# Attention scores on one core: two batches interleaved per transpose, 8 KB load runs, all loads ahead of all stores

## The chip, the cores and the metric

One core of a Trainium2 chip. The metric is device time in microseconds; the profile's span is 1.8 to 2 us shorter. Short names: PE is TensorE, DVE is VectorE, ACT is ScalarE, POOL is GpSimd, SP is SyncE, which here issues all DMAs. A slice of the page is a fortieth of the span, and a digit in it is a busy share in tenths.

## The reference

```python
batch, heads, seq, dim = 8, 8, 512, 64            # q, k: float32
def reference(q, k):
    scale = 1.0 / np.sqrt(q.shape[-1])
    return (np.einsum('bhqd,bhkd->bhqk', q, k) * scale).astype(np.float32)
```

16.78 MB come in, 67.11 MB go out.

## The kernel before

Each batch is loaded, cast to bf16, transposed on TensorE, which puts the 64 dims on the partitions, multiplied and evicted from PSUM with the scale. One transpose takes a 128 x 128 block made of two halves of the heads (index x), 64 dims each, so x later picks the upper or lower 64 rows of TensorE (the profile has the score matmuls as 64*64). Loads run four batches ahead; from then on each batch's stores are mixed with the loads of a later one.

```python
    G = H // 2; M = P // G; R = S // M; RO = 8          # 4, 32, 16
    q_r = q.rearrange("b (x g) (m j) d -> b (g m) x (j d)", x=2, j=R)   # two runs of 4 KB per partition
    raw_pool = ...(name="raw", bufs=4)    # kf and qf, 8 KB each per partition
    bf_pool  = ...(name="bf", bufs=2)     # kb and qb
    t_pool   = ...(name="t", bufs=2)
    out_pool = ...(name="out", bufs=6)    # 16 KB per partition, 2 MB each
    # tpsum: 2 tiles, psum: 3 tiles
    ...
    for b in range(B):
        ... casts of kf, qf (GpSimd; VectorE and ScalarE for the first batch)
        for j0 in range(0, R, 8):
            tp = tpsum_pool.tile([P, 8, P], bf16, name="tp")
            ... 8 transposes of kb into tp
            nc.vector.tensor_copy(out=kT[:, :, j0:j0 + 8], in_=tp.rearrange("d j p -> d p j"))
        ... the same for qb, evicted by ScalarE into qT
        for g0 in range(0, G, 2):
            os = [out_pool.tile([P, 2 // HP, RO, S], f32, name="o") for _ in range(2)]
            ... 32 matmuls (64 rows, 64 columns, 512 wide), evictions by turns on ScalarE and VectorE
            for x in range(2):
                nc.sync.dma_start(out=out_r[b, x, ...], in_=os[x]...)      # 16 KB runs
            if g0 == 0 and b + AHEAD < B:
                load(b + AHEAD)
```

The two tiles written together are called a pair here: 4.19 MB of stores, 16 pairs in all. ScalarE evicts into the first tile of a pair, VectorE into the second.

## Time and profile before

| | before |
|---|---|
| time, median of 3 | 206.02 us (205.98 to 206.03) |
| span | 204.0 us |
| busiest compute engine | TensorE, 63% of the span |
| DMA queue, share of 16 engines' span | 97.6% |
| moved | 83.89 MB in 16 loads and 32 stores |

Read the row of DMA shares first: here it is full from end to end (a 9, that is 90% or more, in 38 of 40 slices), while the busiest compute engine has 63%. So I take the DMA as the bound, and its own rate in GB/s by stage is what counts. The list of DMA issues says how deep the queue is (count, KB each, median us from issue to landing; the line of the stores):

```profile
out_dram<-o SPq DMA_DIRECT2D x32, 2048.0 KB, 24.8
```

A 2 MB store alone takes 4.9 us, by my estimate, at the 430 GB/s of the stretch with stores only (120 to 195 us). At 24.8 us from issue to landing, about five stores are queued at any time. That depth goes with the six output tiles; with the four of the changed kernel its page has 14.4 us, three stores.

### The profile page before, as it was taken

What the parts mean: (1) busy time and instruction counts of PE and PEld (TensorE: products, weight loads), DVE (VectorE), ACT (ScalarE), POOL (GpSimd) and SP (SyncE); (2) the same over time, 40 slices, a digit from 0 to 9 for tenths busy, and PEclk for the clock granted to TensorE, in tenths of its full rate; (3) what the DMA queues carried; (4) which work ended last, traced back from release to release, by engine and by line L of the source; (5) the groups of instructions that cost most, each with busy time, mean ns of one, the idle gap of its engine ahead of it and who ended that gap; (6) DMA issues with size and microseconds to landing.
All of it is one profiled execution on the core that took longest, in us unless ns stands there. A gap on an engine that the chain in (4) does not pass through costs nothing.

```text
span 204.0 us, 1911 instructions
## 1 busy us (share of the span) xinstructions
PE 128.7 (63%) x768; PEld 44.1 (22%) x768; DVE 94.4 (46%) x82; ACT 82.8 (41%) x83; POOL 29.0 (14%) x34
## 2 busy tenths in 40 slices
PE   0398877774969559696586955959787777600000
PEld 0353433260103411033110431103211111000000
DVE  0459895912639035490536705367628081800000
ACT  2477888263522625227252452527552525200000
POOL 1077530520006100070001600000000000000000
PEclk9999999666555855558555575555555555555555
DMA  5999999999999999999999999999999999999991
GB/s 204 419 409 411 439 427 404 441 434 424 437 400 432 440 421 419 434 429 427 440 407 414 438 427 437 427 421 437 424 430 437 426 434 424 430 437 427 434 408 61
DMA packets 8969, 84.01 MB, mean 412 GB/s; under 512 B 768, under 2 KB 768, under 8 KB 4864
## 3 DMA queue, kind: packets, MB, share of 16 engines
q1 hardware_dynamic: 8960, 83.89, 97.6%
q8 instruction: 6, 0.10, 0.2%
q14 instruction: 3, 0.02, 0.0%
HBM read 16.78 MB, written 67.11 MB: 411 GB/s over the span
## 4 chain that ended last, share of the span: by engine, by line
DMA 61%; DVE 14%; PE 6%; ACT 6%; issue 1%; SPq 0%; DVEq 0%
DMA out_dram<-o 57%; DVE o L73 11%; PE ps L119 4%; ACT o L71 4%; DMA qf<-in_q_dram 3%; DVE kT L97 3%; ACT qT L105 1%; PE tp L103 1%; PE tp L95 0%; DVE qb L87 0%; SPq L56 0%; SPq L128 0%; DVEq L73 0%
## 5 line engine op out<-in xcount | busy, mean ns | idle before, releaser
L119 PE MATMUL ps<-kT,qT 64*64 64x512 bf16 x512 | 103.1, 556 | 38.6 <-ACT o L71 24.9
L73 DVE TENSOR_SCALAR o<-ps 128x1024 f32<-128x1024 f32 x64 | 75.2, 1219 | 76.7 <-DMA out_dram<-o 56.8
L71 ACT ACTIVATE o<-ps 128x1024 f32<-128x1024 f32 x64 | 64.5, 1025 | 77.1 <-PE ps L119 65.7
L119 PEld LDWEIGHTS <-qT 64*64 64x64 bf16 x512 | 22.4, 124 | 111.5 <-issue 108.6
L87 POOL CAST kb<-kf 128x1024 bf16<-128x1024 f32 x14 | 14.2, 1040 | 80.9 <-DMA kf<-in_k_dram 80.3
L105 ACT COPY qT<-tp 128x1024 bf16<-128x1024 bf16 x16 | 16.1, 1015 | 12.6 <-PE tp L103 12.4
L97 DVE COPY kT<-tp 128x1024 bf16<-128x1024 bf16 x16 | 18.9, 1215 | 0.0
L95 PE MATMUL tp<-identity,kb 128*128 128x128 bf16 x128 | 12.4, 257 | 8.0 <-ACT kb L87 6.9
L103 PE MATMUL tp<-identity,qb 128*128 128x128 bf16 x128 | 14.9, 284 | 2.2 <-DVE kT L97 1.4
L87 POOL CAST qb<-qf 128x1024 bf16<-128x1024 f32 x14 | 14.2, 1040 | 6.4 <-DMA qf<-in_q_dram 6.4
L103 PEld LDWEIGHTS <-qb 128*128 128x128 bf16 x128 | 11.7, 130 | 9.6 <-issue 8.6
L95 PEld LDWEIGHTS <-kb 128*128 128x128 bf16 x128 | 10.4, 118 | 11.4 <-ACT kb L87 6.9
L87 DVE CAST kb<-kf 128x1024 bf16<-128x1024 f32 x1 | 0.7, 694 | 5.8 <-DMA kf<-in_k_dram 5.8
L87 ACT CAST kb<-kf 128x1024 bf16<-128x1024 f32 x1 | 1.0, 1044 | 3.8 <-DMA kf<-in_k_dram 3.8
L87 ACT CAST qb<-qf 128x1024 bf16<-128x1024 f32 x1 | 1.0, 1044 | 1.5 <-DMA qf<-in_q_dram 1.5
L87 ACT ACT_TABLE_LOAD x1 | 1.3, 1283 | 0.7 <-PEq L147 0.7
L87 DVE CAST qb<-qf 128x1024 bf16<-128x1024 f32 x1 | 0.7, 695 | 1.9 <-DMA qf<-in_q_dram 1.9
masks.py:199 POOL TENSOR_SCALAR_AFFINE_SELECT identity<-identity 128x128 bf16<-128x128 bf16 x1 | 0.3, 292 | 0.1
masks.py:197 POOL MEMSET identity<- 128x128 bf16 x1 | 0.2, 204 | 0.3 <-POOLq L147 0.3
L147 POOL MEMSET const-float32-0.0<- 128x1 f32 x1 | 0.1, 98 | 0.2 <-issue 0.2
L147 POOL MEMSET const-bfloat16-1.0<- 128x1 bf16 x1 | 0.1, 101 | 0.0
L147 POOL MEMSET const-uint8-127<- 128x1 uint8 x1 | 0.1, 101 | 0.0
(1 smaller groups left out, 0.1 us busy)
## 6 DMA issues: line engine op xcount, KB each, us to landing
out_dram<-o SPq DMA_DIRECT2D x32, 2048.0 KB, 24.8
kf<-in_k_dram SPq DMA_DIRECT2D x8, 1024.0 KB, 17.2
qf<-in_q_dram SPq DMA_DIRECT2D x8, 1024.0 KB, 19.6
```

What stands on the lines that cost most here:

```text
L71: nc.scalar.mul(out=dst, in_=src, mul=scale)
L73: nc.vector.tensor_scalar(out=dst, in0=src, scalar1=scale, scalar2=None, op0=mybir.AluOpType.mult)
L87: copy(out=dst[:, :, x, :], in_=slab[:, x].rearrange("p (j d) -> p j d", j=R))
L95: nc.tensor.transpose(out=tp[:, j, :], identity=identity, in_=kb[:, j0 + j].rearrange("p x d -> p (x d)"))
L97: nc.vector.tensor_copy(out=kT[:, :, j0:j0 + 8], in_=tp.rearrange("d j p -> d p j"))
L103: nc.tensor.transpose(out=tp[:, i, jj, :], identity=identity, in_=qb[:, RO * jj + i0 + i].rearrange("p x d -> p (x d)"))
L105: nc.scalar.copy(out=qT[:, i0:i0 + IW], in_=tp.rearrange("d i jj p -> d i p jj"))
L119: nc.tensor.matmul(out=pss[x][h * U:(h + 1) * U, w, :], lhsT=qTh[rows, i + w, g, :], rhs=kTh[rows, g, :], start=True, stop=True, tile_posi ...
L147: nc = _bacc.Bacc("TRN2", target_bir_lowering=False, num_devices=1)
```

## The change

The intent: longer load runs (8 KB instead of two of 4 KB), a queue with all reads ahead of all writes, and the transposed q and k of everything held on chip. To get 8 KB runs, x now means two batches instead of two halves of the heads; two batches are a unit, and there are four units. The memory for this comes from the output tiles, of which 4 are left. Cut to its core:

```diff
-    G = H // 2
+    UNITS = B // 2
+    G = H
-    q_r = q.rearrange("b (x g) (m j) d -> b (g m) x (j d)", x=2, j=R)
+    q_r = q.rearrange("b g (m j) d -> b (g m) (j d)", j=R)
-    raw_pool = ctx.enter_context(tc.tile_pool(name="raw", bufs=4))
-    bf_pool = ctx.enter_context(tc.tile_pool(name="bf", bufs=2))
-    t_pool = ctx.enter_context(tc.tile_pool(name="t", bufs=2))
-    out_pool = ctx.enter_context(tc.tile_pool(name="out", bufs=6))
+    raw_pool = ctx.enter_context(tc.tile_pool(name="raw", bufs=6))
+    bf_pool = ctx.enter_context(tc.tile_pool(name="bf", bufs=3))
+    t_pool = ctx.enter_context(tc.tile_pool(name="t", bufs=UNITS))
+    out_pool = ctx.enter_context(tc.tile_pool(name="out", bufs=4))
... (cast, transposes and matmuls as before, for a unit in place of a batch)
+    cast = [load_and_cast(0)]
+    for v in range(1, UNITS):
+        cast.append(load_and_cast(v))
+
+    ts = [transpose(*cast[0])]
+    scores(0, 0, *ts[0])
+    ts.append(transpose(*cast[1]))
+    scores(0, 1, *ts[0])
+    ts.append(transpose(*cast[2]))
+    ts.append(transpose(*cast[3]))
+    for v in range(UNITS):
+        for n in range(2 if v == 0 else 0, H // 2):
+            scores(v, n, *ts[v])
```

scores(v, n) makes and stores one pair.

More of the change, by code (lines that the diff above doesn't have):

```diff
@@ L30 @@
     RO = 8
-    HP = RO * P // S
-    U = P // HP
+    U = S // RO
     JJ = R // RO
+    IW = 8 // JJ
     f32 = mybir.dt.float32
     bf16 = mybir.dt.bfloat16
-    q_r = q.rearrange("b (x g) (m j) d -> b (g m) x (j d)", x=2, j=R)
-    k_r = k.rearrange("b (x g) (m j) d -> b (g m) x (j d)", x=2, j=R)
-    out_r = out.rearrange("b (x n h) (u i) k -> b x n (h u) i k", x=2, h=HP, i=RO)
+    q_r = q.rearrange("b g (m j) d -> b (g m) (j d)", j=R)
+    k_r = k.rearrange("b g (m j) d -> b (g m) (j d)", j=R)
+    out_r = out.rearrange("b (n h) (u i) k -> b n (h u) (i k)", h=2, i=RO)
     consts = ctx.enter_context(tc.tile_pool(name="consts", bufs=1))
-    raw_pool = ctx.enter_context(tc.tile_pool(name="raw", bufs=4))
-    bf_pool = ctx.enter_context(tc.tile_pool(name="bf", bufs=2))
-    t_pool = ctx.enter_context(tc.tile_pool(name="t", bufs=2))
-    out_pool = ctx.enter_context(tc.tile_pool(name="out", bufs=6))
+    raw_pool = ctx.enter_context(tc.tile_pool(name="raw", bufs=6))
+    bf_pool = ctx.enter_context(tc.tile_pool(name="bf", bufs=3))
+    t_pool = ctx.enter_context(tc.tile_pool(name="t", bufs=UNITS))
+    out_pool = ctx.enter_context(tc.tile_pool(name="out", bufs=4))
     tpsum_pool = ctx.enter_context(tc.tile_pool(name="tpsum", bufs=2, space=bass.MemoryType.PSUM))
     psum_pool = ctx.enter_context(tc.tile_pool(name="psum", bufs=3, space=bass.MemoryType.PSUM))
-    AHEAD = 4
-    raws = {}
-    def load(b):
-        kf = raw_pool.tile([P, 2, R * D], f32, name="kf")
-        qf = raw_pool.tile([P, 2, R * D], f32, name="qf")
-        nc.sync.dma_start(out=kf, in_=k_r[b])
-        nc.sync.dma_start(out=qf, in_=q_r[b])
-        raws[b] = (qf, kf)
-    load(0)
-    identity = consts.tile([P, P], dtype=bf16)
-    make_identity(nc, identity)
-    for b in range(1, AHEAD):
-        load(b)
+    identity = None
     n_evac = 0
@@ L75, in evacuate, with load_and_cast @@
         n_evac += 1
-    for b in range(B):
-        qf, kf = raws.pop(b)
-        kb = bf_pool.tile([P, R, 2, D], bf16, name="kb")
-        qb = bf_pool.tile([P, R, 2, D], bf16, name="qb")
-        for slab, dst in ((kf, kb), (qf, qb)):
+    def load_and_cast(v):
+        both = []
+        for src in (k_r, q_r):
+            xb = bf_pool.tile([P, R, 2, D], bf16, name="xb")
             for x in range(2):
-                if b > 0:
+                xf = raw_pool.tile([P, R * D], f32, name="xf")
+                nc.sync.dma_start(out=xf, in_=src[2 * v + x])
+                if v > 0:
                     copy = nc.gpsimd.tensor_copy
@@ L86, with transpose @@
                     copy = (nc.vector.tensor_copy, nc.scalar.copy)[x]
-                copy(out=dst[:, :, x, :], in_=slab[:, x].rearrange("p (j d) -> p j d", j=R))
+                copy(out=xb[:, :, x, :], in_=xf.rearrange("p (j d) -> p j d", j=R))
+            both.append(xb)
+        return both
+    def transpose(kb, qb):
         kT = t_pool.tile([P, P, R], bf16, name="kT")
@@ L97 @@
             nc.vector.tensor_copy(out=kT[:, :, j0:j0 + 8], in_=tp.rearrange("d j p -> d p j"))
-        IW = 8 // JJ
         for i0 in range(0, RO, IW):
@@ L105, with scores @@
             nc.scalar.copy(out=qT[:, i0:i0 + IW], in_=tp.rearrange("d i jj p -> d i p jj"))
+        return kT, qT
+    def scores(v, n, kT, qT):
         kTh = kT.rearrange("d (g m) j -> d g (m j)", g=G)
         qTh = qT.rearrange("d i (g m) jj -> d i g (m jj)", g=G)
-        for g0 in range(0, G, 2):
-            os = [out_pool.tile([P, 2 // HP, RO, S], f32, name="o") for _ in range(2)]
-            for n in range(2 // HP):
-                for i in range(0, RO, 2):
-                    pss = [psum_pool.tile([P, 2, S], f32, name="ps") for _ in range(2)]
-                    for w in range(2):
-                        for h in range(HP):
-                            g = g0 + n * HP + h
-                            for x in range(2):
-                                rows = slice(x * D, (x + 1) * D)
-                                nc.tensor.matmul(out=pss[x][h * U:(h + 1) * U, w, :],
-                                                 lhsT=qTh[rows, i + w, g, :],
-                                                 rhs=kTh[rows, g, :],
-                                                 start=True, stop=True,
-                                                 tile_position=(x * D, h * U))
-                    for x in range(2):
-                        evacuate(os[x][:, n, i:i + 2, :], pss[x])
-            for x in range(2):
-                n0 = g0 // HP
-                nc.sync.dma_start(
-                    out=out_r[b, x, n0:n0 + 2 // HP].rearrange("n p i k -> p n (i k)"),
-                    in_=os[x].rearrange("p n i k -> p n (i k)"))
-            if g0 == 0 and b + AHEAD < B:
-                load(b + AHEAD)
@@ new lines, in scores @@
+        os = [out_pool.tile([P, RO, S], f32, name="o") for _ in range(2)]
+        for i in range(0, RO, 2):
+            pss = [psum_pool.tile([P, 2, S], f32, name="ps") for _ in range(2)]
+            for w in range(2):
+                for h in range(2):
+                    for x in range(2):
+                        rows = slice(x * D, (x + 1) * D)
+                        nc.tensor.matmul(out=pss[x][h * U:(h + 1) * U, w, :],
+                                         lhsT=qTh[rows, i + w, 2 * n + h, :],
+                                         rhs=kTh[rows, 2 * n + h, :],
+                                         start=True, stop=True,
+                                         tile_position=(x * D, h * U))
+            for x in range(2):
+                evacuate(os[x][:, i:i + 2, :], pss[x])
@@ new lines, in scores @@
+        for x in range(2):
+            nc.sync.dma_start(out=out_r[2 * v + x, n], in_=os[x].rearrange("p i k -> p (i k)"))
+    cast = [load_and_cast(0)]
+    identity = consts.tile([P, P], dtype=bf16)
+    make_identity(nc, identity)
+    for v in range(1, UNITS):
[9 more added lines that the diff above has]
+            scores(v, n, *ts[v])
```

## The prediction

> **What bounds the kernel now.** I read the page's slices first, then the table of stretches, the waits, the timeline of the queue and the chain. Slices:
>
> ```profile
> PE 128.7 (63%) x768; PEld 44.1 (22%) x768; DVE 94.4 (46%) x82; ACT 82.8 (41%) x83; POOL 29.0 (14%) x34
> ...
> PEclk9999999666555855558555575555555555555555
> DMA  5999999999999999999999999999999999999991
> GB/s 204 419 409 411 439 427 404 441 434 424 437 400 432 440 421 419 434 429 427 440 407 414 438 427 437 427 421 437 424 430 437 426 434 424 430 437 427 434 408 61
> ```
>
> No slice between the first and the last has the DMA engines under 90% busy, while no compute engine passes 63% of the span. So the time is the bytes over the rate, plus a start and an end. The table of stretches (us; busy and count of each engine; granted clock; DMA share; GB/s) splits that sum. The first 8 loads are queued by 7 us and no store is issued before 18.89, so 5 to 19 is pure load; the last loads land before 120, so 120 to 195 is pure store:
>
> ```profile
> 0.00:5.00 5.00, 0.00 (x0) 0.00 (x0) 0.00 (x0) 1.28 (x1) 0.70 (x6) 1.00 0.59 201
> ...
> 5.00:19.00 14.00, 9.84 (x94) 6.24 (x97) 9.14 (x9) 8.23 (x9) 6.34 (x7) 1.00 1.02 413
> 120.00:195.00 75.00, 42.97 (x196) 9.85 (x195) 30.53 (x26) 25.67 (x26) 0.00 (x0) 0.52 1.01 430
> ...
> 198.00:199.00 1.00, 0.00 (x0) 0.00 (x0) 0.00 (x0) 0.00 (x0) 0.00 (x0) 0.50 0.73 311
> 199.00:200.00 1.00, 0.00 (x0) 0.00 (x0) 0.00 (x0) 0.00 (x0) 0.00 (x0) 0.50 0.31 131
> 200.00:201.00 1.00, 0.00 (x0) 0.00 (x0) 0.00 (x0) 0.00 (x0) 0.00 (x0) 0.50 0.27 115
> 201.00:202.00 1.00, 0.00 (x0) 0.00 (x0) 0.00 (x0) 0.00 (x0) 0.00 (x0) 0.50 0.08 33
> 202.00:203.00 1.00, 0.00 (x0) 0.00 (x0) 0.00 (x0) 0.00 (x0) 0.00 (x0) 0.50 0.04 16
> ```
>
> Loads, in runs of 4 KB, go at 413 GB/s; stores, in runs of 16 KB, at 430. 16.78 MB / 413 = 40.6 us and 67.11 / 430 = 156.1 us, together 196.7. The start costs 5 - 201 x 5 / 413 = 2.6 us. That leaves 204.0 - 199.3 = 4.7 us of end, and the last five lines are it: the 16 DMA engines don't finish together, the last is about 4 us behind the first.
>
> Compute is kept waiting by the stores, and not the other way round:
>
> ```profile
> DVE o L73 <- DMA out_dram<-o: 56.8, 11, 8.7
> ...
> 59.17 4.73 DVE L73 TENSOR_SCALAR o<-ps 128x1024 f32<-128x1024 f32 x4 [4.95 <-DMA out_dram<-o]
> 60.45 4.75 PE L119 MATMUL ps<-kT,qT 64*64 64x512 bf16 x20 [0.77 <-DVE o L73]
> ```
>
> The first line is of VectorE's waits (total, times, longest), the others of the timeline: when an output buffer comes free, VectorE fills it with 4 evictions in 4.73 us and the store is issued at once (63.68). At the halved clock 20 score matmuls take 4.75 us, so the 32 of a pair of output tiles take about 7.6, against the 9.75 us in which the queue stores that pair (4.19 MB / 430).
>
> [...]
>
> **The change part by part.**
>
> *Load runs.* From 16 loads of two 4 KB runs per partition to 16 loads of one 8 KB run: bytes and loads are the same, runs go from 4096 to 2048. Fit one run on one engine as a fixed part plus bytes over a rate. 4096 x 16 / 413 GB/s = 158.7 ns, 16384 x 16 / 430 GB/s = 609.6 ns; the slope is 450.9 ns per 12288 bytes, the fixed part 158.7 - 150.3 = 8.4 ns. An 8 KB run is then 309 ns (424 GB/s) for two of 158.7, and each engine has 128 of them: 128 x 8.4 = 1.1 us saved. The cut in the sum is 40.6 to 39.5 us. That is all the DMA work that the change removes. The stores keep size, count (32) and run length.
>
> *Order in the queue.* In the built order all 16 loads stand ahead of the first store. Mixing costs nothing now: 20 to 120 moves 42.6 MB, 9.6 of loads and 33.0 of stores, which at 413 and 430 would take 100.0 us and does take 100. So separating them gains nothing either.
>
> *Compute work.* A unit is now two batches transposed together, so there are 4. Casts: the same elements in instructions twice as long (POOL 1040 ns each before, about 2.0 after; the first unit's on VectorE 1.4 and ScalarE 2.1, twice the rows of 694 and 1044 ns). Transposes stay 256, their evictions 32, the score matmuls 512, the evictions 128. Nothing changes there in sum, and none of it is on the path.
>
> *Buffers.* Output tiles go from 6 to 4 and casts from two pairs to 3 singles. These are the new risk, so I place the start by hand, loads landing every 2.47 us from 5.8 (before's first landing): number 8 at 23, 10 at 28, 16 at 43. Do loads ever stall on their 6 buffers? Load 15 needs the cast of load 9 (landed 25.5, cast at 27.5), load 16 that of load 10 (30.0); the engines then are at load 10, so the queue is never under 4 loads deep. Loads end at 5 + (16.78 - 1.0) / 0.424 = 42.2 us. The first store pair is ready at about 28, the second at about 40, both ahead of that; they keep the queue busy to 42.2 + 2 x 9.75 = 61.7 us.
>
> The third pair is the tight spot. In the built order TensorE does the transposes of the third and fourth unit (128) before it goes on with that pair's matmuls, having done only some 16 of 32. With 2 PSUM tiles the transposes run at the pace of their evictions: per unit 4 x 1.22 on VectorE plus 4 x 1.02 on ScalarE, about 0.9 overlapped, 8.1 us. From the end of the second pair's evictions, 39 on VectorE, ScalarE finishes the eighth set of these at about 55.5. Then 3 more rounds of matmuls and evictions at 1.2 to 2 us each (clock between full and half): the first store of the third pair is issued at 61 to 62.5, and before's first load needed about 1 us from issue to its first bytes. First bytes at 62 to 63.5 against 61.7: a gap of 0.3 to 1.8 us, I take 1.2. This is the only idle time of the queue that I find. From the fourth pair on a buffer freed at T gives a new store at T + 4.73 + about 1.2, while the queue has the other pair, 9.75 us: 3.8 us to spare.
>
> *Sum.* 206.0 - 1.1 (runs) + 1.2 (third pair)[...] = 206.2 us.
>
> **Rivals.** (a) No gap: my hand placing is too slow, as it strings waits of two engines end to end, and matmuls at full clock would leave the store in time. The start of the trace speaks for it (clock 1.00 to 30 us). Then only the runs count: 204.9. (b) Better than that: the lag of the slow DMA engines partly comes from short reads, and the 4.7 us end shrinks with half as many. [...] It would give 203 to 204. (c) A new wait: 4 output tiles are too few[...]. [...] Half a microsecond on each of 16 pairs would give 213. (d) These transposes take 4 us longer than placed, at half clock or behind the GpSimd casts into 3 buffers: 209 to 210.
>
> **Range and chances.** The two computed terms cancel, each about 1 us. I put 30% on (a), 10% on (b), 40% on the gap as placed, 13% on (d), 7% on (c). 2% is 4.1 us: faster needs under 201.9, that is the end gone altogether, which nothing here does (0.03). Slower needs over 210.1, (c) or a bad (d): 0.09. Within 2%: 0.88. The range for 8 in 10 is 203.6 to 209.0.
>
> **What would show it.** Runs: a stretch from 5 to 40 us, now pure load, should have 424 GB/s; 413 would mean that run length does nothing. Order: no store issued before 30 us, and loads landing by about 43. Third pair: a dip of DMA share within 60 to 65 us and nowhere else, with VectorE and ScalarE before it busy on the transposes' evictions, not waiting. Buffers: later DMA share 0.99 or more; shares of 0.95 in every pair would prove (c). End: the time from the first thinning of the DMA to the last byte still 4 to 5 us; 2 or less would prove (b). The whole is wrong if another engine than the DMA ends the chain, or if the rate of pure stores leaves 430.

The sum came to 206.2 us. Terms are cut from it: the 0.1 us for the four tiles, which no trace or run shows, so the terms that still stand come to 206.1. The 8.4 ns per run is an estimate, from the trace's 413 and 430 GB/s. For the end the profile shows only the mean share of the 16 engines, 0.73 falling to 0.04 over the last five lines; that some engines lag behind others is my estimate from that (0.04 of 16 engines for 1 us is 0.64 us of work, about one run of 16 KB at the fit's 609.6 ns).

## The result

The changed kernel took 204.58 us (median of 4 runs, 204.37 to 205.21), the kernel before 206.03 in the same rounds. The ratio is 0.9932 (0.9909 to 0.9956). Ratios are the mean time of one kernel's fast runs over that of the other's of the same rounds, so not quite the ratio of the medians quoted. A difference counts only from 2% on. It is 1.45 us less, where 206.2 was forecast.

The page of the changed kernel, slices:

```profile
PE 134.3 (66%) x768; PEld 40.9 (20%) x768; DVE 96.2 (47%) x82; ACT 84.1 (41%) x83; POOL 23.4 (12%) x18
...
PEclk9999999999755555555555555555555555555555
DMA  5999999999999999999999999999999999999991
GB/s 218 431 426 423 418 426 417 420 428 423 439 423 426 436 430 430 433 426 433 426 426 433 428 428 430 436 423 426 433 423 436 431 423 436 426 423 433 433 426 74
```

The DMA row is full as before: the DMA is still the bound, and no gap shows. By stretches (us; busy and count of each engine; granted clock, DMA share, GB/s; shares a few hundredths above 1.00 stand so in the profile and are read as full):

```profile
0.00:5.00 5.00, 0.00 (x0) 0.00 (x0) 0.00 (x0) 1.28 (x1) 0.70 (x6) 1.00 0.58 213
...
5.00:40.00 35.00, 24.59 (x244) 15.17 (x245) 25.23 (x22) 19.38 (x19) 17.55 (x10) 1.00 1.02 424
...
120.00:195.00 75.00, 50.69 (x212) 9.88 (x211) 32.98 (x28) 27.07 (x28) 0.00 (x0) 0.50 1.01 429
...
197.00:198.00 1.00, 0.00 (x0) 0.00 (x0) 0.00 (x0) 0.00 (x0) 0.00 (x0) 0.50 0.88 377
198.00:199.00 1.00, 0.00 (x0) 0.00 (x0) 0.00 (x0) 0.00 (x0) 0.00 (x0) 0.50 0.43 180
199.00:200.00 1.00, 0.00 (x0) 0.00 (x0) 0.00 (x0) 0.00 (x0) 0.00 (x0) 0.50 0.31 131
200.00:201.00 1.00, 0.00 (x0) 0.00 (x0) 0.00 (x0) 0.00 (x0) 0.00 (x0) 0.50 0.08 33
```

The second line is pure load now, at the forecast 424 GB/s. The sum of the prediction, done again with these lines:

| us | before | after |
|---|---|---|
| start, 5 us less what was moved by then | 2.6 | 5 - 213 x 5 / 424 = 2.5 |
| loads | 40.6 | 16.78 / 424 = 39.6 |
| stores | 156.1 | 67.11 / 429 = 156.4 |
| end and gaps, the rest of the span | 4.7 | 202.9 - 198.5 = 4.4 |
| span | 204.0 | 202.9 |

So the loads give 1.0 us, and the 1.2 us that the third pair was to cost is missing. The timeline of that pair, VectorE's line and SP's:

```profile
55.15 4.73 DVE L59 TENSOR_SCALAR o<-ps 128x1024 f32<-128x1024 f32 x4 [6.83 <-DMA out_dram<-o]
```

```profile
59.66 1.61 SPq L117 DMA_DIRECT2D out_dram<-o  x2
```

VectorE had waited 6.83 us for its output tile. The last eviction of the transposes, on ScalarE, ended at 51.9 us and the tile came free at 55.15, so the buffer set the time. The stores went out at 59.66 us, 1.3 us ahead of the earliest time I had placed them at (61), and the queue did not run dry.

### The profile page after: what moved, and what is told of

Its sections match the earlier page's. It is cut to its first block, busy times and chain, and to the rows that moved or that the text cites. A ratio compares the mean times of both kernels' runs of the same rounds, so it can differ in the third digit from the quotient of the medians.

```text
span 202.9 us, 1888 instructions
## 1 busy us (share of the span) xinstructions
PE 134.3 (66%) x768; PEld 40.9 (20%) x768; DVE 96.2 (47%) x82; ACT 84.1 (41%) x83; POOL 23.4 (12%) x18
## 3 DMA queue, kind: packets, MB, share of 16 engines
HBM read 16.78 MB, written 67.11 MB: 413 GB/s over the span
## 4 chain that ended last, share of the span: by engine, by line
DMA 61%; DVE 12%; PE 8%; ACT 7%; SPq 2%; issue 1%; DVEq 0%
DMA out_dram<-o 57%; DVE o L59 9%; PE ps L109 6%; ACT o L57 5%; DMA xf<-in_q_dram 4%; DVE kT L88 2%; ACT qT L95 2%; PE tp L93 2%; SPq L117 1%; PE tp L86 1%; DVE xb L75 1%; SPq L70 0%; DVEq L59 0%
## 5 line engine op out<-in xcount | busy, mean ns | idle before, releaser
L109 PE MATMUL ps<-kT,qT 64*64 64x512 bf16 x512 | 113.5, 584 | 35.2 <-ACT o L57 29.5
L109 PEld LDWEIGHTS <-qT 64*64 64x64 bf16 x512 | 23.2, 127 | 120.4 <-issue 117.8
L75 POOL CAST xb<-xf 128x2048 bf16<-128x2048 f32 x12 | 22.7, 1895 | 23.2 <-DMA xf<-in_k_dram 18.1
L86 PE MATMUL tp<-identity,xb 128*128 128x128 bf16 x128 | 11.3, 241 | 13.2 <-ACT xb L75 10.1
L95 ACT COPY qT<-tp 128x1024 bf16<-128x1024 bf16 x16 | 15.6, 1016 | 10.3 <-PE tp L93 10.1
L93 PE MATMUL tp<-identity,xb 128*128 128x128 bf16 x128 | 10.7, 235 | 3.5 <-DVE kT L88 1.7
L86 PEld LDWEIGHTS <-xb 128*128 128x128 bf16 x128 | 9.0, 108 | 17.1 <-ACT xb L75 10.1
L93 PEld LDWEIGHTS <-xb 128*128 128x128 bf16 x128 | 8.7, 105 | 6.9 <-issue 5.7
L75 ACT CAST xb<-xf 128x2048 bf16<-128x2048 f32 x2 | 3.8, 1897 | 9.2 <-DMA xf<-in_k_dram 6.1
L75 DVE CAST xb<-xf 128x2048 bf16<-128x2048 f32 x2 | 2.5, 1228 | 9.4 <-DMA xf<-in_k_dram 5.6
```

What stands on the lines that cost most here:

```text
L75: copy(out=xb[:, :, x, :], in_=xf.rearrange("p (j d) -> p j d", j=R))
L86: nc.tensor.transpose(out=tp[:, j, :], identity=identity, in_=kb[:, j0 + j].rearrange("p x d -> p (x d)"))
L93: nc.tensor.transpose(out=tp[:, i, jj, :], identity=identity, in_=qb[:, RO * jj + i0 + i].rearrange("p x d -> p (x d)"))
L95: nc.scalar.copy(out=qT[:, i0:i0 + IW], in_=tp.rearrange("d i jj p -> d i p jj"))
L109: nc.tensor.matmul(out=pss[x][h * U:(h + 1) * U, w, :], lhsT=qTh[rows, i + w, 2 * n + h, :], rhs=kTh[rows, 2 * n + h, :], start=True, stop ...
```

## The experiments

### The yardstick again, and a surprise

The changed kernel as it is, on another chip.

> The changed kernel again, as the yardstick for the others on this chip. Both theories: 204.6 us (0.993 of before), pure loads at 424 GB/s in the stretch 5 to 40 us.

Measured: 208.37, 208.28, 207.23, 204.61, 208.28 and 204.19 us, against 205.73 to 206.12 for the 11 runs of the kernel before among them. Two executions are as fast as in the first measurement; four are slower than the kernel before. Three of those count as slow and are outside the ratio (0.9969; 0.9919 to 1.0019); the one of 207.23 still counts as fast and is in it. But the kernel before, run by turns on the same chip, has no such runs, so I looked into the trace of one (208.37 us). Third pair, stretches:

```profile
60.00:61.00 1.00, 0.80 (x4) 0.13 (x4) 1.00 (x1) 0.15 (x1) 0.00 (x0) 0.66 0.92 393
61.00:62.00 1.00, 0.18 (x2) 0.00 (x0) 0.16 (x1) 0.79 (x1) 0.00 (x0) 0.50 0.51 213
62.00:63.00 1.00, 0.71 (x8) 0.42 (x10) 0.00 (x0) 0.24 (x1) 0.00 (x0) 0.50 0.12 49
63.00:64.00 1.00, 1.00 (x8) 0.22 (x2) 0.61 (x1) 0.00 (x0) 0.00 (x0) 0.50 0.10 33
64.00:65.00 1.00, 0.54 (x4) 0.13 (x3) 1.00 (x2) 0.80 (x1) 0.00 (x0) 0.50 0.00 0
65.00:66.00 1.00, 1.00 (x10) 0.35 (x9) 0.74 (x1) 0.22 (x1) 0.00 (x0) 0.50 0.00 0
```

This is the gap of the prediction, at the place it named, and larger: summed over these lines the queue is idle for 4.35 us (6 less the shares). The pair's first store is issued at 65.25 us instead of 59.66. Why so late? TensorE's timeline in the fast execution (the first measurement's), and then in this slow one, at the same two groups of its program (4 score matmuls, then 8 transposes):

```profile
29.46 0.62 PE L109 MATMUL ps<-kT,qT 64*64 64x512 bf16 x4
30.02 0.62 PE L93 MATMUL tp<-identity,xb 128*128 128x128 bf16 x8
```

```profile
33.94 1.06 PE L109 MATMUL ps<-kT,qT 64*64 64x512 bf16 x4
34.93 1.03 PE L93 MATMUL tp<-identity,xb 128*128 128x128 bf16 x8
```

The same work takes 1.7 times as long. In the fast execution the short times begin at 19.3 us, in the slow one at 39.9; until then TensorE runs at half clock, as I call the long times: 1.06 us for 4 score matmuls is also what they take where the column of the granted clock shows 0.50 (at 58.62 us in the kernel before). Here that column shows 1.00 for both; the durations decide. So the traces have two states and a moment that varies. What sets the moment they do not show: in the slow execution TensorE is busy for 18.99 of the 20 us from 20 to 40 us, and still at half clock until 39.9. By then its transposes are 6 us late (the same 8 of line 93 begin at 39.87 us instead of 33.44), and the third pair inherits that. VectorE's line for the third unit's k, fast and then slow, shows where the block of 128 transposes ahead of the third pair begins:

```profile
35.78 4.61 DVE L88 COPY kT<-tp 128x1024 bf16<-128x1024 bf16 x4
```

```profile
42.22 4.61 DVE L88 COPY kT<-tp 128x1024 bf16<-128x1024 bf16 x4
```

From there to the last eviction of the block on ScalarE it is 16.1 us in both (to 51.9 and to 58.3 us): by then TensorE is at full clock in both, and only the beginning moves. This is theory A; the rival B is a slow state of the chip.

### TensorE warmed

```diff
+    wide = consts.tile([P, S], dtype=bf16)
+    nc.vector.memset(wide, 1.0)
+    busy(30)            # 30 matmuls identity x wide into a PSUM tile that nobody reads
...
-    ts = [transpose(*cast[0])]
+    ts = [transpose(*cast[0], keep=2)]     # and busy(2) after each 8 transposes of the first unit
```

The scheduler also orders the first units' matmuls and transposes a little differently for it.

> The changed kernel with TensorE kept busy from the start: 30 idle matmuls of 512 columns before the first load has landed and 2 after each group of 8 transposes of the first unit, results unused. Theory A (the slow executions of the changed kernel, 208.3 us, come from TensorE running at half clock until 40 us, so that the third pair of stores is issued after the queue has run dry): all executions at 204.2 to 205.2 us, none above 206, and in the profile 8 transposes in about 0.6 us from 20 us on and no dip of the DMA at 61 to 66 us. Rival B (a slower state of the chip or of its memory, whatever the kernel): still two groups of times, 204.5 and 208.3.

Measured: 204.15 to 204.65 us in 4 runs, 0.9916 of before (0.9903 to 0.993). TensorE's timeline, with transposes of the first unit at full clock from their start (the changed kernel took 1.89 for its first 16):

```profile
10.01 0.61 PE L91 MATMUL tp<-identity,xb 128*128 128x128 bf16 x8
```

and the stretch of 61 to 66 us has a DMA share of 1.00. No slow execution; but four fast ones in a row the changed kernel had had too. So both went together to another chip:

> The changed kernel again, beside the warmed one on the same chip. Theory A (whether TensorE leaves half clock at about 19 us or at about 40 us is decided anew in each execution): executions of both kinds, some at 204.2 to 205.2 us, some at 207 to 208.5. Rival B (a matter of the chip): all of one kind.

> The warmed kernel again, on that same chip. Theory A: every execution at 204.1 to 205.2 us, also where the changed kernel has slow ones. Rival B: as many slow ones as the changed kernel.

Measured: the changed kernel 204.22 to 204.59 us in 5 runs, ratio 0.9921 (0.9908 to 0.9933); the warmed one 204.30 to 204.46 in 4, ratio 0.992 (0.9906 to 0.9933). No slow execution in either, so this pair didn't separate A from B: it shows only that warming costs nothing where nothing is slow. In all, the changed kernel was fast in 11 of 15 executions, with all four others on one chip, which the warmed kernel never met. Why that chip so often stays at half clock is open.

### The third pair made late on purpose

What can be settled without that chip is whether a late third pair makes such times. With TensorE warmed, the evictions of the transposed k were done twice, for the fourth unit (4 x 1.22 us more on VectorE), then for the third and fourth:

```diff
-            nc.vector.tensor_copy(out=kT[:, :, j0:j0 + 8], in_=...)
+            for _ in range(1 + again):
+                nc.vector.tensor_copy(out=kT[:, :, j0:j0 + 8], in_=...)
...
-    ts.append(transpose(*cast[3]))
+    ts.append(transpose(*cast[3], again=1))     # in the second run also for cast[2]
```

> The warmed kernel with each eviction of the fourth unit's transposed k done twice: 4 x 1.22 = 4.9 us more on VectorE ahead of the third pair, TensorE at full clock. Theory A (the third pair being late, not the clock as such, makes the slow executions): the third pair's first store comes some 4 us later, the DMA dips at 61 to 65 us in every execution, 206.0 to 207.5 us. Rival (the clock or another state makes them slow): 204.5 us, as the evictions are off the path.

> The warmed kernel with the evictions of both the third and the fourth unit's transposed k done twice: 9.8 us more on VectorE ahead of the third pair. With half of that the first store of the third pair came 2.2 us later (61.9 against 59.7 us) and the time rose by 0.6 us; in the slow execution of the changed kernel it came at 65.3 us and the time rose by 3.7. Theory A: here it comes at about 66 us, with TensorE at full clock at 20 to 45 us, and every execution takes 208 to 210 us, like the slow ones. Rival (half clock of itself, or another state, makes the slow ones): 204.3 to 205.5 us.

Measured: 204.51 to 204.97 us (5 runs; ratio 0.9943) and 206.64 to 206.87 us (5 runs; ratio 1.0034). SP's timeline for the third pair, one line from each of the two:

```profile
61.89 1.61 SPq L127 DMA_DIRECT2D out_dram<-o  x2
```

```profile
63.84 0.81 SPq L127 DMA_DIRECT2D out_dram<-o  x2
```

Stretches of the second, with the gap:

```profile
61.00:62.00 1.00, 1.00 (x12) 0.77 (x14) 1.00 (x1) 0.12 (x1) 0.00 (x0) 0.53 0.50 213
62.00:63.00 1.00, 0.47 (x8) 0.11 (x1) 0.59 (x2) 1.00 (x2) 0.00 (x0) 1.00 0.19 82
63.00:64.00 1.00, 0.13 (x4) 0.13 (x7) 0.78 (x1) 0.82 (x1) 0.00 (x0) 1.00 0.04 16
64.00:65.00 1.00, 0.92 (x12) 0.30 (x8) 0.41 (x1) 0.42 (x1) 0.00 (x0) 1.00 0.62 262
```

Both expectations were too high in size, and the first time is nearer to the rival's 204.5 than to theory A's 206.0. In the second, the stores came at 63.84 us and not at 66, because the scheduler put matmuls of the third pair ahead of the last transposes. Nor was TensorE at full clock to the end of the block: 8 transposes take 1.03 us again from 46.8 us on in the first and from 39.0 us on in the second. But set side by side by when the third pair's first store is issued, the four make one curve:

| third pair's first store issued, us | time, us | over the first row |
|---|---|---|
| 59.58 (warmed) | 204.33 | |
| 61.89 (evictions of one unit twice) | 204.92 | 0.6 |
| 63.84 (of two units) | 206.74 | 2.4 |
| 65.25 (slow execution of the changed kernel) | 208.37 | 4.0 |

The times of the first three rows are medians of runs that agree within 0.5 us, the issue of the store is from the one profile of each; the last row is one execution. The rows come from three chips (the first two share one), and on the chip of the last the fast executions took 204.4. In the first three TensorE has full clock from 11 to 35 us at least, where the slow execution has half clock; a late third pair costs time all the same, in every execution, and the slow execution lies where its own lateness puts it. Half clock alone, on the other hand, need not cost anything: in the profile of the kernel with 1 KB runs (below) TensorE is at half clock until 41.6 us too, but the loads last longer there, the third pair is still in time (DMA share 0.99 from 61 to 66 us), and this execution's 210.71 us are the median of its five. I take this as showing what the slow executions lose their time to. That half clock made them late is read from one trace, not produced at will.

The curve starts flat: 2.3 us of lateness cost 0.6. The queue's idle time in that run is 0.61 + 0.27 + 0.11 = 1.0 us from 61 to 64 us, of which 0.4 did not reach the end. Where it went is not shown. What goes with it is a shorter end: in the changed and the warmed kernel three lines of 1 us stand there with a share between 0.04 and 0.7 (as 0.43, 0.31, 0.08 above), in the three executions with a late pair only two (0.35 and 0.08 from 200 us, 0.24 and 0.08 from 202 us, 0.66 and 0.15 from 203 us). That some engines run ahead of others and use up their lead in the gap is my guess from these shares; the profile shows only the mean of 16 engines.

### Run length

```diff
-                xf = raw_pool.tile([P, R * D], f32, name="xf")
-                nc.sync.dma_start(out=xf, in_=src[2 * v + x])
+                C = R * D // 2                        # for the 1 KB runs, 8 in place of each 2
+                xf = raw_pool.tile([P, 2, C + 16], f32, name="xf")
+                nc.sync.dma_start(out=xf[:, :, :C], in_=src[2 * v + x].rearrange("p (s c) -> p s c", s=2))
... (the casts read the pieces; their count and elements are as before)
```

> The changed kernel with each load landing in two 4 KB runs per partition instead of one of 8 KB (a gap of 64 bytes in the tile splits them); all else as after. Theory 1 (the run length makes the gain, 8.4 ns for each run on each of 16 engines): 128 more runs per engine, +1.1 us, so 205.7 us, about the time of before, and 5 to 40 us at 413 GB/s. Rival (the order, all loads before all stores, makes it): stays at 204.6 us.

> The same with eight 1 KB runs per partition: 896 more runs per engine than after. Theory 1, if the fixed part is the same at every length: 896 x 8.4 ns = +7.5 us, 212.1 us, loads at about 356 GB/s. [...] Rival (order): 204.6 us. If short runs also make the DMA engines drift apart, the end (first thinning of the DMA to the last byte) grows beyond after's 4 us.

Measured, on the chip of the yardstick: 205.23 to 205.91 us for 4 KB (median 205.5, ratio 0.9979, 0.9967 to 0.9991) and 210.65 to 210.81 for 1 KB (median 210.71, ratio 1.0231). The stretch of pure loads, 4 KB and then 1 KB:

```profile
5.00:40.00 35.00, 24.99 (x212) 14.69 (x213) 21.50 (x19) 19.21 (x18) 16.95 (x9) 0.90 1.03 415
```

```profile
5.00:40.00 35.00, 25.89 (x171) 14.17 (x172) 18.91 (x16) 15.80 (x15) 14.19 (x8) 1.00 1.09 368
```

Against the fast executions of the yardstick (204.19 and 204.61, mean 204.4) a run costs (205.5 - 204.4) / 128 = 8.6 ns per engine at 4 KB and (210.7 - 204.4) / 896 = 7.0 ns at 1 KB. The prediction's fit had 8.4. With only two fast executions to compare with, 0.4 us apart, the first figure is good to some 2 ns, so that it comes so close is in part luck. At 1 KB the 6.3 us are 1.2 under the 7.5 that the expectation had from the fit (a second estimate there is cut, as nothing measured here gave it). The rival, order alone, would have left both at 204.6 and fails. But the 4 KB kernel is still 0.55 us under the kernel before, so run length is not the whole gain. The end did not grow with short runs: at 1 KB it has two such thin lines (0.35 and 0.15, from 205 us), and that without a gap before, so a late pair is not all that can shorten it. (TensorE came to stay at full clock only at 32.4 us in the profile of the 4 KB kernel, with a DMA share of 0.97 over 60 to 75 us; without that the 4 KB kernel might be a little faster, and its cost per run smaller.)

### Order in the queue

```diff
-    for v in range(1, UNITS):
+    for v in range(1, UNITS - 1):
         cast.append(load_and_cast(v))
...
     scores(0, 0, *ts[0])
+    cast.append(load_and_cast(UNITS - 1))
```

> The changed kernel with the loads of the fourth unit (4 of 16) queued behind the first pair of stores instead of ahead of all stores; run length stays 8 KB. Theory 1 (order is worth nothing): 204.6 us within 0.4. Rival (order makes the gain): at least a quarter of 1.45 us comes back, 205.0 us or more.

> The warmed kernel with the fourth unit's 4 loads behind the first pair of stores, as in the run with the late loads (204.93 us, on another chip, 0.4 over the changed kernel's fast executions). If order is worth something even for a quarter of the loads: 0.3 to 0.5 us over the warmed kernel. If order is worth nothing, as predicted: within 0.2 us of it.

Measured: 204.67 to 205.87 us (median 204.93, 6 runs), ratio 0.9954; and from the warmed kernel 204.73 to 204.99 (5 runs), ratio 0.9943, beside 204.30 to 204.46 for the warmed kernel itself on the same chip. The second is the clean comparison: the ranges don't touch, and the medians are 0.43 us apart. Putting a quarter of the loads behind stores costs that much, where I had said nothing. The stretch of 20 to 40 us, warmed kernel and then with the late loads, looks like the place (1% less over 20 us is 0.2 us):

```profile
20.00:40.00 20.00, 16.17 (x184) 9.58 (x185) 17.90 (x16) 12.78 (x14) 13.91 (x8) 1.00 1.01 420
```

```profile
20.00:40.00 20.00, 16.15 (x184) 9.62 (x185) 17.92 (x16) 12.77 (x14) 11.36 (x6) 1.00 1.01 416
```

But it is made up for at once: from 40 to 60 us the late kernel has 431 GB/s against 424, and by 195 us it has moved 82.28 MB against 82.19. It is nowhere behind from 60 to 195 us, and still its span is 0.5 us longer. In the profile of the first late kernel, though, 0.25 MB are missing at 40 us already (15.63 MB against 15.88 of the changed kernel) and stay so. So the 0.43 us are shown, and where they are lost is not.

The first late kernel ran on the chip with the slow executions and had none in 6. In the built order of both, the fourth unit's transposes come after the third pair instead of before it, so they don't have the tight spot, and differ from their yardsticks in that as well.

### Three output tiles

`out` with bufs=3 instead of 4.

> The changed kernel with 3 output tiles instead of 4. By the prediction's sum, a buffer freed at T gives a new store's first bytes at T + 4.73 + 1.2 = T + 5.9. With 4 tiles the queue then has 9.75 us of work, with 3 only one tile of 2 MB, 4.9 us: a gap of about 1.0 us on each of some 14 pairs, +14 us, 219 us, and DMA shares of 0.9 in the second half. If the slack were wrongly reckoned and 3 tiles were enough: 204.5 us; if the two engines' fills can't overlap the store at all: +60 us or more.

Measured: 224.61 to 226.54 us (4 runs), ratio 1.0937 (1.0901 to 1.0972). The DMA row of its page:

```profile
DMA  6999999995989697979797979797979796979797
```

Every pair now has a dip. (225.4 - 204.4) / 14 = 1.5 us per pair, where 1.0 was reckoned from T + 5.9 against 4.9 us of queue. (The 204.4 are from another chip, where the kernel before took 0.2 us less.) The reckoning left out that TensorE is held up too: in VectorE's waits for this run 54.8 us in 10 waits are for the matmuls' results, against 42.9 us in 7 for output tiles. So the slack that the prediction saw with 4 tiles is real, and with one tile less it is gone.

### Fewer instructions on TensorE

Wrong result: units 2 to 4 use the first unit's kT and qT, so their transposes and the evictions of these are left out.

```diff
-    ts.append(transpose(*cast[1]))
+    ts.append(ts[0])           # and so for the third and fourth unit
```

> Wrong result on purpose: the transposes of units 2 to 4 are left out (all scores from the first unit), so TensorE's program has 1154 instead of 1538 instructions and the third pair is ready early; all loads, casts, evictions and stores as after. Theory C (the 4 us of end are made by the instruction fetches, which each take one DMA engine 1 us from its stores): one or two fetches fewer than the 6 of after, the end about 1 us shorter, 203.3 to 204.0 us. Rival (the end has another source): 204.5 us, the end as long as after's. Theory A: no slow executions.

The 1 us for a fetch is an estimate from the page of the changed kernel: 6 fetches took 0.2% of 16 engines' 202.9 us, 1.1 us each; that it is lost to the stores is the theory's guess.

Measured: 203.83 to 204.30 us (5 runs, median 203.95), ratio 0.9898, beside 204.53 for the warmed kernel on the same chip. The page counts 4 instruction fetches instead of 6. The stretches of the end, warmed kernel and then this one:

```profile
198.00:199.00 1.00, 0.00 (x0) 0.00 (x0) 0.00 (x0) 0.00 (x0) 0.00 (x0) 0.50 0.43 180
199.00:200.00 1.00, 0.00 (x0) 0.00 (x0) 0.00 (x0) 0.00 (x0) 0.00 (x0) 0.50 0.27 115
200.00:201.00 1.00, 0.00 (x0) 0.00 (x0) 0.00 (x0) 0.00 (x0) 0.00 (x0) 0.50 0.12 49
```

```profile
198.00:199.00 1.00, 0.00 (x0) 0.00 (x0) 0.00 (x0) 0.00 (x0) 0.00 (x0) 0.50 0.31 131
199.00:200.00 1.00, 0.00 (x0) 0.00 (x0) 0.00 (x0) 0.00 (x0) 0.00 (x0) 0.50 0.19 82
200.00:201.00 1.00, 0.00 (x0) 0.00 (x0) 0.00 (x0) 0.00 (x0) 0.00 (x0) 0.50 0.04 16
```

0.6 us less, at the edge of what was expected, but the end is as long as before, only thinner. This doesn't show that fetches make the end, and it doesn't exclude it. What makes the end stays open.

## Why the prediction was right, and where it was not

- **The bound.** Right: the DMA row is full before and after (a 9 in 38 of 40 slices), and the stores keep 429 to 430 GB/s.
- **Run length, -1.1 us.** Right in mechanism and size: 424 GB/s as forecast, and splitting the runs again costs 1.1 us (4 KB) and 6.3 us (1 KB).
- **Order in the queue, 0.** Wrong by about 0.4 us. "Separating them gains nothing" rested on a sum over 100 us, in which 0.4 us are 0.4%: less than 2 GB/s in the two rates, and so finer than I could read it; and it took the end as fixed. Putting a quarter of the loads back among the stores costs 0.43 us. For all that the change does beside run length, the order of all mixed loads and the tiles together, the 4 KB kernel gives 0.55 us (206.05 less 205.5).
- **Third pair, +1.2 us.** Right as a place and in the pace of the transposes, wrong in when they begin. The block took 16.1 us where I had 16.5 (39 to 55.5). But I let it begin at 39 us, as if that were one moment; in the traces it moves with the moment of full clock: 35.8 us in the fast execution, where the output tile then came last, the store went out at 59.66 and nothing was lost; 42.2 us in the slow one, with the store at 65.25 and some 4 us lost. The 39 lies between, and one profile is there: the 4 KB kernel, at full clock for good from 32.4 us, with the block from 39.8 to 55.9, the store at 62.43 and a DMA share of 0.92 from 61 to 66 us, much as I had placed it. My sum was off too: 55.5 and three rounds of 1.2 to 2 us are 59.1 to 61.5, not 61 to 62.5; in the slow execution the rounds took 6.9 us in all. And I quoted "clock 1.00 to 30 us" as support, from a column that reads 1.00 in the slow execution while its transposes take 1.03 us. The fast executions are rival (a), to which I gave 30% and 204.9; the slow ones are rival (d), with 13% and 209 to 210.
- **Four tiles are enough.** Right from the fourth pair on: a DMA share of 1.01 and 429 GB/s over 65 to 195 us. Rival (c) needs three tiles to come true.
- **The end, 4.7 us.** It stayed (4.4), against rival (b); that eight times as many reads, of 1 KB each, did not lengthen it speaks against (b) too.
- **The total.** 204.58 lies in the range, 1.6 us under the centre. That is the third pair's 1.2 and the order's 0.4: two misses of the same sign, which the range was wide enough to hold.
- **A reading.** The store at 63.68 us that I quoted as VectorE's is that of ScalarE's tile (its last eviction ends at 63.65); VectorE's fill ends at 63.90. The argument stands without it.

The slow executions, 207.2 to 208.4 us, lie in the range as well. With them the change is a loss on the chip where they came: 206.8 us in the mean of six, against 206.0. The warmed kernel was level with the changed kernel's fast executions where both ran (204.33 and 204.35 us), 0.992 of before on two chips, with no slow execution in 8. It has yet to be run on that chip.

## What to carry to other kernels

In a kernel bound by its DMA queue, reckon the time as bytes over rate by stage, and then look for the one place where the queue can run dry: here it was the end of a block of loads, with a long stretch of transposes ahead of the next store. If compute there depends on TensorE's clock state, place it twice, for the earliest and the latest moment of full clock (here 19.3 and 39.9 us), not with a mean. And run such a kernel on more than one chip before calling it faster: four equal runs on one did not show what six on another did.
